# One modulation segment of a two-layer mixer and MoE kernel, made in the routing of layer 0 instead of between its gates

## The chip, the cores and the metric

The kernel runs on one core of one Trainium2 chip. The metric is the device time of one execution in microseconds; three executions of the kernel before are given, and one profiled execution, from which all rows are read. The engines are PE (TensorE; PEld is its weight load), DVE (VectorE), ACT (ScalarE), POOL (GpSimd) and SP (SyncE, whose queue issues most of the loads).

## The reference, cut to what matters

Two layers work on 512 latent tokens and 256 context tokens of width 1024. In each, adaptive modulation rows (six segments of 1024, one row for the latent tokens and one for the context) shift, scale and gate what the layer does.

```python
for l in range(2):
    with_ctx = l < 1
    mod   = silu(c)     @ w_mod[l] + b_mod[l]      # w_mod[l] is 1024 x 6144
    mod_c = silu(c_ctx) @ w_mod[l] + b_mod[l]
    sh1, sc1, gt1, sh2, sc2, gt2 = split(mod, 6)   # csh1 ... cgt2 likewise
    h, hc = modulate(x, sh1, sc1), modulate(ctx, csh1, csc1)
    y = sum(sigmoid(h @ w_gate[n] + b_gate[n]) * (branch_n(h @ w_in) @ w_branch[n])
            for n in A, B, C, D) @ w_out           # four kinds of attention
    x = x + gt1 * y                                # with_ctx: the same for ctx
    h2 = modulate(x, sh2, sc2)
    x = x + gt2 * hier_moe(h2)                     # 32 experts, 2 for each token
return rmsnorm(x)
```

Segment (1, 5) of the kernel is `gt2` of layer 1, the gate on its mixture of experts. It is read only when layer 1 combines its experts. The context row of layer 1 is needed for the segments 0 and 1 alone.

## The kernel before

Both layers are one program, run stage by stage: the norm and the first two modulation segments (to about 45 us), the attention branches and gates of layer 0 (to 820 us), its merge, output projection and routing (to 945), its experts (to 1260), and the same for layer 1.

In the attention stage two streams of work go into one instruction order. The main items are the branches, in the order B, A, C, D: loads of `w_in`, splits of each weight tile into a high part `wH` on ACT and a low part `wL` on DVE (lines 278 and 279), projections, scores, softmax, transposes (line 259). The other stream, `gates()`, fills in: 32 columns of gates, each with a 512 KB load of `w_gate` (line 288), a split, 24 matmuls for each token group, a tanh, and a store of `th` (line 1252). A planner, `Flow`, models the engines and chooses at each step between a main item and the next piece of fill; of the fill it takes so much that its modelled work stays under `FILL` times that of the main items (0.8 in layer 0, 0.4 in layer 1). Its choices are fixed before the kernel runs: each engine executes its list in order.

At every odd column `gates()` first makes a modulation segment with `mod_seg(l, q, new)`: a load of the bias row into a tile `mrow` (line 400), eight loads of `w_mod` of 512 KB each into tiles `wmod` (line 405), for each of them four matmuls of 256 columns, with the two silu columns as weights, replicated to 32 (line 254: `mat`; the four run in separate column groups of the array), a DVE addition of the bias (line 413), and writes of the row to a DRAM tile `modd` by POOL's queue (line 418). Between two of the eight groups the planner may put main work. The tiles come from the pool `gslot`, six buffers that the gates share.

The output projection has its own `Flow`, with ratio 0.0. For each tile of 128 tokens it makes four quarters of the projection, transposes, router logits (`post`), and after every three tiles `route`, which picks experts and counts them. Its weights and the merged rows are in the pool `slot`, 30 buffers. The last of `route` writes indices (`at`, L1909, then the owners' weights, L1921), and `overflow_list` counts the experts whose tokens exceed 64 (`nbb`, `ovJ`, `ovv`, `ovvb`; L1727 to L1753) into `LE`, `LR` and `nover`. A hardware loop then runs from `nover`, and its entry waits for all engines and queues. 26 expert tiles `e` are loaded ahead of it (L1699, also from `slot`). After it the experts run in pairs (L1782).

Of the kernel before, what the change touches and what calls it, by code (L numbers as in the profile page):

```python
# [19 lines left out]
D = 1024  # L20
# [125 lines left out]
class Flow:  # L146
# [13 lines left out]
    def use(self, cls, after):  # L160
        self.used.append((cls, after))
# [74 lines left out]
class Build:  # L236
# [157 lines left out]
    def mod_seg(self, l, q, new, use=None):  # L394

        nc = self.nc
        sl = self.gslot(name="mrow")
        bias, row = sl[:, :256], sl[:, 256:512]
        b = self.a["b_mod"][l, q * D:(q + 1) * D]
        nc.sync.dma_start(bias, bass.AP(tensor=b.tensor, offset=b.offset, ap=[[256, 4], [0, 32], [1, 256]]))  # L400
        yield 0.0, ("bk",)
        ps = self.bank()
        for k in range(8):
            w = new(name="wmod")
            nc.sync.dma_start(w, self.a["w_mod"][l, q, k])
            for g in range(4):
                self.mat(ps[32 * g:32 * g + 32, :256], self.sc[:, k, :], w[:, g * 256:(g + 1) * 256],
                         start=k == 0, stop=k == 7, tile_position=(0, 32 * g))
            if k < 7:
                yield self.LT["mod"], ()  # L410
        if self.fl:
            self.fl.use("bk", self.LT["gacc"])
        nc.vector.tensor_tensor(row, ps[:, :256], bias, op=ALU.add)
        if use:
            use(row)
        else:
            for g in range(4):
                nc.gpsimd.dma_start(self.modd[l][:, q * D + g * 256:q * D + (g + 1) * 256],
                                    row[32 * g:32 * g + 2, :])

    def mix_rows(self, l):

# [109 lines left out]
    def dense(self, x, sh, A):  # L532

        f = self.fl = Flow(NSLOT - 14 if self.l else NSLOT - 10, FILL[self.l])
        if self.l == 0:
# [689 lines left out]
    def gates(self):  # L1225
        nc, l, f = self.nc, self.l, self.fl
        bg = self.tiny.tile([128, 4, 8], F32, name="bg", tag="bg")
        nc.gpsimd.dma_start(bg, self.a["b_gate"][l])
        hb = self.tiny.tile([128, 4, 8], F32, name="hb", tag="hb")
        nc.vector.tensor_scalar(hb, bg, 0.5, None, op0=ALU.mult)  # L1230
        segs = [(0, q) for q in range(2, 6)] + [(1, q) for q in range(6)] if l == 0 else []
        for i in range(32):
            n, m = ORDER[i // 8], i % 8
            if segs and i % 2 == 1:
                yield from self.mod_seg(*segs.pop(0), self.gslot)
            H, L = self.load_split(self.a["w_gate"][l, n, m].rearrange("p k n -> p (k n)"), self.gslot, eng=GE and nc.gpsimd)
            v = lambda s: s.rearrange("p (k n) -> p k n", k=8)
            H, L = v(H), v(L)
            for t0, tn in [(0, 512), (512, 256)][:1 + self.wc]:
                yield 0.0, ("bk", "norms") if t0 else ("bk",)  # L1240
                G = self.bank()
                for k in range(8):
                    a, b = (self.hsl(z, k, t0, tn) for z in range(2))
                    for x, y in ((H, a), (H, b), (L, a)):
                        self.mat(G[:, :tn], x[:, k], y, start=k == 0 and y is a and x is H,
                                 stop=k == 7 and x is L)
                    if k < 7:
                        yield 0.0, ()
                f.use("bk", self.LT["gacc"])
                th = self.sm.tile([128, 512], F32, name="th", tag="th", bufs=2)  # L1250
                nc.scalar.activation(th[:, :tn], G[:, :tn], AF.Tanh, scale=0.5, bias=hb[:, n, m:m + 1])  # L1251
                nc.sync.dma_start(self.thd[n][m, :, t0:t0 + tn], th[:, :tn])
            self.gate[8 * n + m].done, self.gate[8 * n + m].t = True, f.clk
        self.give(12)
# [87 lines left out]
    def out_proj(self):  # L1342
        nc, l = self.nc, self.l
        f = self.fl = Flow(NSLOT, 0.0)
# [31 lines left out]
        def quarter(i, t):  # L1376
            W, x, cs = self.wo[i], self.x1[t], slice(i * 256, (i + 1) * 256)
            ps = self.bank()
            terms = [(ysl(0, k, t), ysl(1, k, t), W(0, k), W(1, k)) for k in range(8)]
            early = i == 0 and t in order[:4]  # L1380
            if early:
                self.mm3(ps[:, :256], terms[:4], True, False)
                f.use("bk", 9000.0)
                yield 3600.0, ()
                b = f.busy["bk"]
                b[b.index(max(b))] = f.clk
            else:
                self.mm3(ps[:, :256], terms[:4], True, False)
            f.use("bk", self.LT["x"])
            self.mm3(ps[:, :256], terms[4:], False, True)  # L1390
            tmp = self.t1("xtmp")
            nc.vector.tensor_tensor(tmp, ps[:, :256], gt1[t // 4][:, cs], op=ALU.mult)
            nc.vector.tensor_tensor(x[:, cs], x[:, cs], tmp, op=ALU.add)

        def turn(t):
            hT[t] = self.gslot(name="xT").rearrange("p (k n) -> p k n", k=8)
            h2, ss = part[t] = self.gslot(name="h2"), self.tiny.tile([128, 2], F32, name="ss2", tag="ss2", bufs=2)
            tp = self.sps()
            f.use("S", self.LT["h2T"])
            for k in range(6):  # L1400
                self.tr(tp[:, k * 128:(k + 1) * 128], self.x1[t][:, k * 128:(k + 1) * 128])
            nc.scalar.activation(hT[t][:, 0:6], tp[:, :768].rearrange("p (k n) -> p k n", k=6), AF.Copy)
            nc.scalar.activation(h2[:, :768], self.x1[t][:, :768], AF.Square, scale=1.0 / 32.0, accum_out=ss[:, 0:1])
            return
            yield
# [11 lines left out]
        def post(t, lt):  # L1417
            x, r = self.x1[t], t // 4
            h2, ss = part[t]
            nc.scalar.activation(h2[:, 768:], x[:, 768:], AF.Square, scale=1.0 / 32.0, accum_out=ss[:, 1:2])  # L1420
            rs = self.rstd(ss[:, 0:1], 1, add=ss[:, 1:2])
            if not H2L:
                norm2(t, h2, rs)
            yield self.LT["x2"], ("bk",)
            tp = self.transposed([x[:, k * 128:(k + 1) * 128] for k in (6, 7)])
            f.use("bk", self.LT["tps"])
            nc.scalar.activation(hT[t][:, 6:8], tp, AF.Copy)
            yield self.LT["h2"], ("bk",)
            lg = self.bank()
            f.use("bk", self.LT["tps"])  # L1430
            for k in range(8):
                self.mat(lg[:, :36], hT[t][:, k], wA[r][:, k], start=k == 0, stop=k == 7)
            nc.vector.scalar_tensor_tensor(lt, lg[:, :36], rs[:, 0:1], cst[r], op0=ALU.mult, op1=ALU.add)
            if H2L:
                norm2(t, h2, rs)
# [12 lines left out]
        for n in RB[l]:  # L1448
            lt = self.sm.tile([128, n, 36], F32, name="lt", tag="lt")
            posts = []  # L1450
            for i in range(n):
                u = order[t + i]
                q3 = f.item(quarter(3, u), deps=[load], need=("bk",))
                tr = f.item(turn(u), deps=[q2[u]], lat=self.LT["x1"], need=("S",))
                posts.append(f.item(post(u, lt[:, i]), deps=[tr, q3, con]))
                f.items += ([] if QM else [q2[u]]) + [tr, q3, posts[-1]]
            t += n
            f.items.append(f.item(self.route(t - n, n, lt, t == self.nt), deps=posts))
        f.run()
        self.fl = None  # L1460

# [513 lines left out]
class Half:  # L1975
# [43 lines left out]
    def v(self, j, t):  # L2019
        return self.V[:, t, 0:64] if self.kind == "g" else self.V[:, t, 64 * j:64 * j + 64]  # L2020
# [15 lines left out]
NT2 = 3  # L2036
GE = False
UPOOL = (3,)
FILL = (0.8, 0.4)
WINDOW = 80  # L2040
ORDER = (1, 0, 2, 3)
PEX = 2
# [27 lines left out]
```

## Time and profile before

| | us |
|---|---|
| three runs | 2195.0, 2189.59, 2190.14 (median 2190.14) |
| the profiled execution | 2185.97 |
| its span, from the first to the last record | 2184.2 |
| granted TensorE clock over the span | 0.97 of 2.4 GHz |
| PE busy | 2020.9 (93%) |

The profiled execution is 4.17 us under the median, and its span leaves out 1.8 us of it. A granted clock of 1.0 in a window is the level of 2.4 GHz, 0.5 that of 1.2 GHz; a value between tells how much of the window had which.

### The profile page before, as it was taken

How to read it: one execution, taken by the hardware profiler on the slowest of the kernel's cores; microseconds unless marked ns; L12 is line 12 of the kernel's file. 1: busy time of each engine (PE TensorE's matmuls, PEld its weight loads, DVE VectorE, ACT ScalarE, POOL GpSimd, SP SyncE). 2: the span in 40 equal slices, each digit the busy share in tenths (PEclk: the TensorE clock that was granted, in tenths of full speed). 3: DMA queues.
4: the chain of work that ended last, by engine and by line, in shares of the span. 5: the costliest groups of instructions: out<-in, count | busy, mean ns of one | idle time of the engine just before them, and what ended most of it. 6: DMA issues, size and time to landing. Idle time of an engine off the chain costs nothing. (4 is left out here: it accounts for less than half of the span.)

```text
span 2184.2 us, 33259 instructions
## 1 busy us (share of the span) xinstructions
PE 2020.9 (93%) x12573; PEld 1483.2 (68%) x12573; DVE 1255.9 (58%) x2695; ACT 799.1 (37%) x1825; POOL 249.8 (11%) x291
## 2 busy tenths in 40 slices
PE   5999999998999998879999979999999999699997
PEld 3878778777788888834444468877877779644443
DVE  3465444245553564677777766565465476656555
ACT  4454554344453221212222235565455432211122
POOL 1101000011100132330000031000020001200000
PEclk8999999999999999889999989999999999799999
DMA  7453542543334656679999423212222478799991
GB/s 285 148 180 102 169 163 81 172 130 100 126 92 134 204 191 212 242 257 393 369 366 365 174 78 100 63 57 88 63 66 77 135 250 288 243 392 409 410 405 68
DMA packets 152931, 428.48 MB, mean 196 GB/s; under 512 B 31488, under 2 KB 43152, under 8 KB 152768
## 3 DMA queue, kind: packets, MB, share of 16 engines
q1 hardware_dynamic: 139744, 392.79, 50.7%
q0 software_dynamic: 11584, 28.29, 4.0%
q10 hardware_dynamic: 1440, 5.24, 0.6%
q8 instruction: 101, 1.65, 0.3%
q14 instruction: 62, 0.51, 0.1%
HBM read 396.28 MB, written 36.78 MB: 198 GB/s over the span
## 5 line engine op out<-in xcount | busy, mean ns | idle before, releaser
L254 PE MATMUL bk<-hT,wH 128*128 128x512 f32 (+1 forms) x1824 | 501.2, 362 | 3.5 <-ACT wH L278 3.1
L254 PEld LDWEIGHTS bk<-hT,wH 128*128 128x128 f32 x1824 | 314.0, 190 | 54.6 <-issue 9.7
L254 PE MATMUL bk<-hT,wL 128*128 128x512 f32 (+1 forms) x912 | 325.6, 357 | 6.9 <-DVE wL L279 6.9
L1841 DVE TENSOR_TENSOR x<-x,sps 128x1024 f32<-128x1024 f32 x166 | 195.4, 1217 | 100.4 <-PE sps L1840 99.8
L1782 PE MATMUL bk<-e,xT 128*64 128x512 f32 x1056 | 245.0, 602 | 0.0
L279 DVE TENSOR_TENSOR wL<-wraw,wH 128x1024 fp32r<-128x1024 f32 (+1 forms) x128 | 157.4, 1234 | 93.6 <-ACT wH L278 59.0
L254 PE MATMUL bk<-wH,hT 128*128 128x256 f32 (+1 forms) x960 | 203.2, 301 | 5.6 <-ACT wH L278 3.6
L254 PEld LDWEIGHTS bk<-hT,wL 128*128 128x128 f32 x912 | 172.9, 190 | 35.2 <-DVE wL L279 10.3
L278 ACT ACTIVATE wH<-wraw 128x1024 fp32r<-128x1024 f32 (+1 forms) x132 | 137.8, 1048 | 136.2 <-DMA wraw<-in_w_gate_dram 45.1
L1782 PEld LDWEIGHTS bk<-e,xT 128*64 128x64 f32 x1056 | 71.9, 138 | 142.3 <-issue 124.0
L254 PEld LDWEIGHTS bk<-wH,hT 128*128 128x128 f32 x960 | 160.7, 194 | 8.5 <-ACT wH L278 3.8
L1840 PE MATMUL sps<-yeH,to 128*128 128x512 f32 x332 | 142.1, 428 | 2.8 <-ACT yeH L278 1.4
L254 PE MATMUL bk<-wL,hT 128*128 128x256 f32 (+1 forms) x480 | 143.0, 298 | 0.8 <-DVE wL L279 0.7
L1203 ACT ACTIVATE P<-sps,m 128x768 f32<-128x768 f32 (+3 forms) x160 | 117.7, 737 | 58.2 <-DVE m L1184 43.5
L1221 ACT ACTIVATE pt<-bk 128x384 f32<-128x384 f32 (+1 forms) x288 | 112.5, 436 | 67.7 <-PE bk L259 66.3
L1840 PE MATMUL sps<-yeL,to 128*128 128x512 f32 x332 | 131.2, 395 | 1.7 <-DVE yeL L279 1.7
L259 PE MATMUL bk<-ident,P 128*128 128x128 f32 x720 | 111.4, 279 | 21.7 <-ACT pt L1221 13.7
L1805 PE MATMUL bk<-e,gT 128*64 128x512 f32 x528 | 122.2, 605 | 1.5 <-ACT gT L1798 1.5
L1788 ACT ACTIVATE eth<-bk 128x256 f32<-128x256 f32 x33 | 12.7, 385 | 284.8 <-PE bk L1782 284.8
L1251 ACT ACTIVATE th<-bk,hb 128x512 f32<-128x512 f32 x96 | 59.1, 616 | 155.9 <-PE bk L254 149.6
L259 PEld LDWEIGHTS bk<-ident,P 128*128 128x128 f32 x720 | 81.9, 140 | 50.5 <-ACT pt L1221 22.8
L325 POOL TENSOR_TENSOR rr<-rs,mhalf 128x1 f32<-128x1 f32 (+1 forms) x72 | 52.0, 723 | 547.1 <-DVE rs L321 476.8
(358 smaller groups left out, 3572.8 us busy)
## 6 DMA issues: line engine op xcount, KB each, us to landing
e<-in_w_dram SPq DMA_DIRECT2D x384, 512.0 KB
wmod<-in_w_mod_dram SPq DMA_DIRECT2D x96, 512.0 KB
wraw<-in_w_gate_dram SPq DMA_DIRECT2D x64, 512.0 KB
thd<-th SPq DMA_DIRECT2D x64, 256.0 KB
wraw<-in_w_in_dram SPq DMA_DIRECT2D x28, 512.0 KB
thm<-thd SPq DMA_DIRECT2D x32, 384.0 KB
wraw<-in_w_br_dram SPq DMA_DIRECT2D x16, 512.0 KB
wraw<-in_w_out_dram SPq DMA_DIRECT2D x16, 512.0 KB
```

The source lines that it names most:

```text
L254: return self.nc.tensor.matmul(out, lhsT, rhs, **kw)
L259: return self.nc.tensor.transpose(out, src, self.ident if ident is None else ident)
L278: nc.scalar.activation(H, src, AF.Copy)
L279: (eng or nc.vector).tensor_tensor(L, src, H.bitcast(F32), op=ALU.subtract)
L325: self.nc.gpsimd.tensor_tensor(r[:, :n], o[:, :n], self.mhalf.to_broadcast([128, n]), op=ALU.pow)
L1203: nc.scalar.activation(Pt[:, :n], S[:, lo:768], AF.Exp, scale=-1.0, bias=m, accum_out=sm)
L1221: nc.scalar.activation(PT[gi][:, i0:i0 + w, qi * 128:(qi + 1) * 128], v, AF.Copy)
L1251: nc.scalar.activation(th[:, :tn], G[:, :tn], AF.Tanh, scale=0.5, bias=hb[:, n, m:m + 1])
L1782: nc.tensor.matmul(box["h"][64 * z:64 * z + 64, :], xT(k, z), W(z, k // 2)[:, (k % 2) * 512:(k % 2 + 1) * 512], start=k == 0, stop=k == 7, ...
L1805: nc.tensor.matmul(Y[n][64 * z:64 * z + 64, :], gT[:, k, 64 * z:64 * z + 64], W(z, 4 + k)[:, n * 512:(n + 1) * 512], start=k == 0, stop=k ...
L1840: nc.tensor.matmul(ps[:, c], to[s, t * 128:(t + 1) * 128], w[s, c], start=i == 0, stop=i == 1)
L1841: nc.vector.tensor_tensor(self.x1[t] if out is None else out, self.x1[t], ps, op=ALU.add)
```

## The change

Segment (1, 5) leaves the list of `gates()`, which now makes nine segments in layer 0, not ten. The output projection of layer 0 gets one item more: the same segment, after the last `route`, with its tiles from `slot`. The writes of a row to `modd` are issued as one DMA with four pieces of 1 KB for each row in place of four DMAs with two rows each, and for layer 1 only the rows that are read later: 16 issues in the program (eight for layer 0, four for the segments 0 and 1 of layer 1 and four for its segments 2 to 5) where 40 stood. `FILL` of layer 0 goes from 0.8 to 0.787.

```diff
@@ mod_seg
         if use:
             use(row)
         else:
-            for g in range(4):
-                nc.gpsimd.dma_start(self.modd[l][:, q * D + g * 256:q * D + (g + 1) * 256],
-                                    row[32 * g:32 * g + 2, :])
+            dst = self.modd[l][:, q * D:(q + 1) * D].rearrange("r (g n) -> r g n", g=4)
+            for r in range(2 if l == 0 or q < 2 else 1):
+                nc.gpsimd.dma_start(dst[r], row[r:128:32, :])
@@ gates
-        segs = [(0, q) for q in range(2, 6)] + [(1, q) for q in range(6)] if l == 0 else []
+        segs = [(0, q) for q in range(2, 6)] + [(1, q) for q in range(5)] if l == 0 else []
@@ out_proj
             f.items.append(f.item(self.route(t - n, n, lt, t == self.nt), deps=posts))
+        if l == 0:
+            f.items.append(f.item(self.mod_seg(1, 5, self.slot), deps=posts))
         f.run()
@@ constants
-FILL = (0.8, 0.4)
+FILL = (0.787, 0.4)
```

Lines behind the second edit carry numbers two higher in the changed kernel. In the rows below a name's number tells one buffer from the next, and `x` with a number counts equal instructions in a row.

The first place is SP's queue among the gates of layer 0, where the last segment's tiles are loaded: `wmod` are its weights, `wraw<-in_w_in` a tile for the branches, `wraw<-in_w_gate` one for a gate column, `o` the store of an attention output. Before:

```order
L405 DMA wmod<-in_w_mod_dram 128x1024 x2
L288 DMA wraw<-in_w_in_dram 128x1024
L1147 DMA o_451<-oT 128x256
L405 DMA wmod<-in_w_mod_dram 128x1024 x2
L288 DMA wraw<-in_w_in_dram 128x1024
L288 DMA wraw<-in_w_gate_dram 128x1024 x3
```

and the same store with its neighbours after the change:

```order
L288 DMA wraw<-in_w_gate_dram 128x1024
L1252 DMA thd_464<-th 128x256
L288 DMA wraw<-in_w_in_dram 128x1024
L1147 DMA o_451<-oT 128x256
L288 DMA wraw<-in_w_in_dram 128x1024
L1252 DMA thd_464<-th 128x512
```

The two `wmod` loads that stood between the store of `o` and the next `w_in` tile are gone; the `w_in` tile follows the store at once.

The second place is PE's list at the end of the routing, from the last indices to the loop (`at` is the assignment matrix, `pt2` and `wp` what it is multiplied with, `nover` the loop's bound in a register). Before:

```order
L1909 MATMUL bk_9816<-pt2_8740,at_9575 128x2
...
L1921 MATMUL bk_9914<-wp_8743,at_9575 128x6
L1733 LDWEIGHTS trib_369
L1733 MATMUL bk_9943<-nbb_9941,trib_369 32x64
L1748 LDWEIGHTS oneb_75
L1748 MATMUL bk_9957<-ovvb_9955,oneb_75 128x72
L1608 TENSOR_LOAD nover_9813
```

and after:

```order
L1911 MATMUL bk_9766<-pt2_8663,at_9498 128x2
L254 MATMUL bk_9689<-wmod_9793,silu_81 32x256 x4
...
L254 MATMUL bk_9689<-wmod_9811,silu_81 32x256 x4
L1923 LDWEIGHTS at_9498
L1923 MATMUL bk_9890<-wp_8666,at_9498 128x6
...
L1735 MATMUL bk_9919<-nbb_9917,trib_369 32x64
L1750 LDWEIGHTS oneb_75
L1750 MATMUL bk_9933<-ovvb_9931,oneb_75 128x72
L1610 TENSOR_LOAD nover_9763
```

The last four of the segment's eight groups, 16 matmuls, have come between the last indices and the chain over `nbb` and `ovvb` that ends in the loop's bound; the first four stand further up, three behind the last router logits and one ahead of the last indices.

The third place is DVE's list at the same point (`nb` and `nbb` count the overflow, `ovJ` is made from PE's product with `nbb`, `w` are the owners' weights). Before:

```order
L1729 TENSOR_REDUCE nb_9939<-ovF_9937 32x1
L1731 CAST nbb_9941<-nb_9939 32x64
L1735 TENSOR_SCALAR ovJ_9945<-iota_367,bk_9943 32x11
L1736 TENSOR_TENSOR ovJ_9945<-ovJ_9945,ovF_9937 32x11
```

and after:

```order
L1731 TENSOR_REDUCE nb_9915<-ovF_9913 32x1
L1733 CAST nbb_9917<-nb_9915 32x64
L413 TENSOR_TENSOR mrow_9687<-bk_9689,mrow_9687 128x256
L1928 TENSOR_REDUCE w_9897<-bk_9890 64x1 x2
L1737 TENSOR_SCALAR ovJ_9921<-iota_367,bk_9919 32x11
L1738 TENSOR_TENSOR ovJ_9921<-ovJ_9921,ovF_9913 32x11
```

The bias addition of the segment, and two reductions that stood further up, have come between `nbb` and `ovJ`.

## Rows read from the trace of the kernel before

**Rows 1.** The page's span line and PE's, DVE's, ACT's, POOL's busy time.
```profile
span 2184.2 us, 33259 instructions
...
PE 2020.9 (93%) x12573; PEld 1483.2 (68%) x12573; DVE 1255.9 (58%) x2695; ACT 799.1 (37%) x1825; POOL 249.8 (11%) x291
```

**Rows 2.** Windows: PE, PEld, DVE, ACT, POOL busy; granted clock; DMA share; GB/s.
```profile
45.00:820.00 775.00, 740.26 (x5065) 611.25 (x5064) 390.71 (x931) 341.37 (x825) 83.84 (x114) 0.98 0.43 142
820.00:945.00 125.00, 95.07 (x780) 92.33 (x781) 74.10 (x196) 23.09 (x55) 36.58 (x37) 0.84 0.60 209
```

**Rows 3.** Timeline of PE, 318 to 322 us: start, duration, line, out<-in, count.
```profile
318.86 0.38 PE L259 MATMUL bk<-ident,dup 128*128 128x128 f32 x2
319.08 0.38 PE L259 MATMUL bk<-ident,qr 128*128 128x128 f32 x2
319.39 0.64 PE L254 MATMUL bk<-wmod,silu 128*32 128x256 f32 x8
319.96 0.44 PE L259 MATMUL bk<-ident,dup 128*128 128x128 f32 x2
```

**Rows 4.** Timeline of PE, modulation matmuls back to back, before 46 us.
```profile
26.48 2.92 PE L254 MATMUL bk<-wmod,silu 128*32 128x256 f32 x48
...
34.45 4.75 PE L254 MATMUL bk<-wmod,silu 128*32 128x256 f32 x32 [1.11 <-DMA wmod<-in_w_mod_dram]
```

**Rows 5.** Tile wmod, 545 to 576 us: min/median/max ns, first and last start.
```profile
L254 PE MATMUL bk<-wmod,silu x64: 379/403/636, 547.8 to 573.0; 128*32 128x256 f32 x64
```

**Rows 6.** Around 561 us: SP's issues, ACT's split, PE's wait (sum, times, longest).
```profile
555.93 0.89 SPq L405 DMA_DIRECT2D wmod<-in_w_mod_dram  x2
556.87 0.42 SPq L288 DMA_DIRECT2D wraw<-in_w_in_dram  x1
...
564.02 1.06 ACT L278 ACTIVATE wH<-wraw 128x1024 fp32r<-128x1024 f32 x1 [2.06 <-DMA wraw<-in_w_in_dram]
...
PE bk L254 <- ACT wH L278: 3.6, 1, 3.6
```

**Rows 7.** Waits of PE, 480 to 505 us: sum, times, longest.
```profile
PE bk L254 <- DMA wmod<-in_w_mod_dram: 3.1, 3, 1.5
PE bk L254 <- ACT wH L278: 1.6, 1, 1.6
```

**Rows 8.** Windows, with the columns of rows 2.
```profile
502.00:506.00 4.00, 3.89 (x20) 3.71 (x21) 1.80 (x5) 2.00 (x4) 0.00 (x0) 0.60 0.10 33
562.00:571.00 9.00, 5.12 (x26) 3.55 (x26) 3.76 (x6) 2.81 (x4) 0.80 (x1) 0.62 0.32 107
...
904.00:913.00 9.00, 8.12 (x49) 8.12 (x49) 4.11 (x14) 2.59 (x8) 0.72 (x1) 0.62 0.17 61
921.00:946.00 25.00, 8.04 (x76) 5.64 (x77) 19.98 (x86) 2.84 (x10) 8.20 (x8) 0.52 0.50 183
```

**Rows 9.** Timeline of PE, end of the routing to the first experts.
```profile
936.46 0.23 PE L1733 MATMUL bk<-nbb,trib 32*32 32x64 bf16 x1 [1.66 <-DVE nbb L1731]
939.26 0.24 PE L1748 MATMUL bk<-ovvb,oneb 32*128 32x72 bf16 x1 [2.57 <-DVE ovvb L1746]
...
942.21 1.97 PE L1690 MATMUL bk<-ident,xg 128*128 128x128 f32 x8 [2.71 <-issue]
944.11 7.78 PE L1782 MATMUL bk<-e,xT 128*64 128x512 f32 x32
```

**Rows 10.** Tiles mrow and modd by line; timeline of POOL.
```profile
L413 DVE TENSOR_TENSOR mrow<-bk,mrow x12: 415/421/426, 32.4 to 573.7; 128x256 f32<-128x256 f32 x12
...
L418 POOL DMA_DIRECT2D modd<-mrow x40: 499/503/824, 93.7 to 576.1; - x40
...
188.78 2.02 POOL L418 DMA_DIRECT2D modd<-mrow  x4
```

**Rows 11.** Timeline of SP's queue, the expert loads ahead of the loop.
```profile
851.95 10.90 SPq L1699 DMA_DIRECT2D e<-in_w_dram  x6
...
875.80 44.11 SPq L1699 DMA_DIRECT2D e<-in_w_dram  x20
```

## The prediction, made before the changed kernel ran

> **What bounds the kernel now.** The page first [rows 1]: PE is busy for 2020.9 of 2184.2 us, and no other engine comes near that. So the next view is the time in which PE is not busy, by stage [rows 2]. In the attention and gates of layer 0 (45 to 820 us) PE is busy for 740.26 of 775.00 us at a granted clock of 0.98: it is the bound there, what is taken from its list shortens the stage, and only 34.7 us of idle time lie in it. In the merge's end, the output projection and the routing (820 to 945) it is busy for 95.07 of 125.00 at 0.84: 29.9 us idle, most of it behind the router's chain on DVE. The change carries work from the first of these stages into the second. Whether that pays is a question about two places: what a group of modulation matmuls costs between other work at 550 us, and whether it fits into idle time of PE at 922 to 942.
>
> **a) Eight groups leave the gates.** The timeline of PE at 319 us gives the price of one group that stands alone [rows 3]. Two transposes start at 318.86, two more at 319.08, so two take 0.22. After the pair at 319.08 the next transposes would start at 319.30; with a group of modulation matmuls between, they start at 319.96, 0.66 later. (The group's eight records are two for each of its four matmuls.) The eight groups of segment (1, 5) lie between 547.8 and 573.0, 64 records [rows 5], with other work between them, so 8 x 0.66 = 5.3 us. Back to back they would be cheaper: 48 records, six groups, take 2.92 us [rows 4], and less the 0.64 of one group [rows 3] that is 2.28 for five, 0.456 each, 3.6 for eight. The groups here are apart, so I take **-5.3**; bounds -3.6 and -5.3.
>
> **b) The stall that the segment's loads make.** Around 561 us PE waits 3.6 us for a split `wH`, ACT itself waited 2.06 us for the load of that `w_in` tile, and SP issued this load at 556.87, right behind two `wmod` loads of 0.89 us [rows 6]. They belong to segment (1, 5), and in the new order of SP's queue (the first place above) none stands there. The load took 564.02 - 556.87 = 7.15 us; with 1 MB less ahead of it, it should be in time or nearly so. ACT's 2.06 us is what a load can be blamed for; the rest of PE's wait is ACT and the score chain. After the wait PE ran at a granted clock of 0.62 from 562 to 571, 5.12 us busy [rows 8]: at most half of it, 2.6 us, was lost to the low level. I take **-2.0**; bounds 0 (something else holds PE there) and -4.7 (2.06 + 2.6).
>
> **c) The segment in the routing.** PE's new list (the second place) puts three groups behind the last router logits and one ahead of the last indices, where PE waits for DVE: 17 of the 25 us from 921 to 946 are idle [rows 8]. These four cost nothing while their loads are there. They are eight loads of 512 KB issued right behind the four of `w_out`, far ahead of 922. The other four groups stand between the last indices and `nbb`'s matmul, on the chain to the loop. The timeline [rows 9]: PE took `nbb` at 936.46 after 1.66 us idle, so it was free at 934.80. Four groups at the low clock take 4.75 us [rows 4], and low it is: 0.52 from 921 to 946 [rows 8]. They end at 939.55, 3.1 behind 936.46. DVE then adds the bias, 0.42 us [rows 10], ahead of `ovJ` (the third place): 3.5. Everything behind moves with it: `ovvb` (2.57 us of waiting), `nover`, the loop's entry, the first experts' transposes at 942.21. So **+3.5**. Bounds: at full clock four groups take 4 x 0.456 = 1.8, of which 1.66 are idle anyway, +0.2 and the 0.42 of the addition, **+0.6**; or the 1.66 are not there, because the matmuls wait for a tile, +4.75 without an overlap, **+4.8**. A tile is the less likely trouble: its buffers come free when the output projection has read `w_out`.
>
> The bias load waits in SP's queue for a tile of `gslot`, and behind it stand the last ten expert loads. Before, 26 were issued from 851.95 to 919.9 [rows 11]. Those ten now go out only near 922 and later, and some wait for the tiles of `wmod` themselves. What covers this: layer 0 starts with the pair at 944.11 [rows 9], which needs the first tiles, not the last; and the loop's entry holds everything until 942. I take **0**. If the cover went, the price would be one tile's issue and landing late, under 7.15 us by the load of [rows 6].
>
> **d) Fewer writes.** The 40 issues cost POOL 0.503 us each [rows 10]; 24 fewer are 12 us of POOL, which is busy for 11% of the span [rows 1]. It is hidden, but for work of POOL that queues behind four in a row (2.02 us at 188.78 [rows 10]); PE there has other work. **0**, at best -1. The write's new shape is not in the trace; its result is read much later, except for segments 0 and 1 of layer 0, which don't go this way.
>
> **e) The new order of the stage.** With `FILL` at 0.787 and a segment less, the planner's list for the whole stage is another one. Nothing in it is more or less work; what can differ is the number of places where a load or a split is late. The trace shows one such cluster, at segment (1, 4): from 480 to 505 us PE waits 3.1 us for `wmod` and 1.6 for a split [rows 7], and then runs at 0.60 for 3.89 busy us [rows 8], of which 40% or 1.6 us is lost: 6.3 us in all. I take **0**, with ends of -6.3 and +6.3 for one cluster less or more. This term is the widest, and I have no row that would decide its sign.
>
> **The sum**: -5.3 - 2.0 + 3.5 + 0 + 0 + 0 = -3.8. Against the profiled execution (2185.97, a span of 2184.2 and 1.8 around it) that is 2182.2. The median of the runs shown is 4.2 above that execution, so for a median I forecast 2190.1 - 3.8 = **2186.3**. About 0.3%, 6.6 us, is what a measurement of this kernel can tell from no change; the forecast lies within it.
>
> **The rivals.**
> *One starved cluster less* (chance 0.30). The places at 485 and 561 us both have `wmod` loads ahead of something urgent [rows 6, 7]; a list with a segment less and a lower ratio may let the first of them vanish too. Then -3.8 - 6.3 = -10.1: 2180.0. Against it: the ratio falls by under 2%, and segment (1, 4) is still there.
> *The routing takes it all back* (0.17). The stall at 561 stays in another form (0 for b), and the four groups cost their full 4.75: -5.3 + 4.75 = -0.6, 2189.6. For it speaks that the chain from `nbb` to the loop has no slack at all [rows 9].
> *Two new starved clusters* (0.11), the one on the other side. Two columns of gates whose split comes late, as at 561 [rows 6], with b) gained nowhere: -5.3 + 3.5 + 2 x 6.3 = +10.8, 2200.9. It decides from 6.6 + 1.8 = 8.4 us of new stall on; one cluster alone gives +4.5. Against it: in 775 us PE now idles only 34.7 [rows 2].
> *The clock wakes in the routing* (0.08). From 921 to 946 PE is granted 0.52, and a window from 904 on shows 0.62 though PE is busy for 8.12 of 9.00 us in it [rows 8]. Were the 16 matmuls enough to bring back 2.4 GHz, the transposes and the first expert matmuls from 942.21 to 946 would run at the high level: at most half of 3.8, 1.9 us. The sum would be -5.7, 2184.4. Beside this: the Trainium skill ("TensorE: Matmul & The Clock Gate", its part on the HAM clock gate) says that sustained work of PE brings the full clock and idling takes it away. The trace agrees that it falls with idling; that it would rise for so short a piece, the rows of 904 to 913 speak against.
>
> The forecast itself, within 3 us or so of 2186.3, has 0.34.
>
> **How the numbers follow.** Faster by over 0.3%: the cluster less, 0.30, and some of the forecast where b) and c) fall to their good ends (-5.3 - 4.7 + 0.6 = -9.4), 0.04: 0.34. Slower by over 0.3%: 0.11. The rest, 0.55, is no change that can be told. The range has to leave out no more than 0.2: below it goes past the cluster less (2180.0) by the difference of b)'s bounds, some 4, to 2176; above past the lost gain (2189.6) by one cluster of 6.3 and a little, to 2197, which leaves out the slower rival. The forecast's own range is 2181 to 2190: the sum with the bounds of b) and c) in it, -9.4 to -0.5.
>
> **What the changed kernel's profile would show.** For a): the columns around 550 to 570 us without modulation matmuls, and the stage shorter by about 5. For b): no wait of 3.6 for `wH` there, idle time of PE from 45 to 820 near 31 and not 35. For c): 16 modulation matmuls (32 records) that start when the last indices have been taken, at a granted clock near 0.5, 4.7 us long; `nbb`'s matmul no longer idle before it, and 4.7 to 5.2 us from the last indices to it, not 1.7; the first expert 3.5 us later after the last indices than before. For the expert loads: no wait of PE for `e`. For e): the sum of PE's waits in the stage; new ones over 1 us for `wH`, `wmod` or `P` say that the list moved the starved places. The prediction is wrong if that sum differs by more than 6 us, if the four groups are not in the way of `nbb`, or if the last expert loads hold up the first pairs.

## The result

| | us | ratio to before, 95% interval |
|---|---|---|
| before, four runs | 2190.28 (2189.59 to 2195.0) | |
| the changed kernel, four runs | 2203.72 (2200.63 to 2209.81) | 1.0066 (1.0049 to 1.0083) |
| its profiled execution | 2200.63, span 2198.8 | |

The change made the kernel 13.4 us slower; 2186.3 was forecast, with a range to 2197. Over all its runs beside the experiments the kernel before took between 2180.2 and 2196.9 us, so a few microseconds of any single profile are chance. Where the time went is therefore read by stages, over all kernels of the study.

The page of the changed kernel answers to [rows 1]: the span and the busy time of each engine.

```profile
span 2198.8 us, 33194 instructions
...
PE 2031.7 (92%) x12573; PEld 1491.6 (68%) x12573; DVE 1255.4 (57%) x2695; ACT 796.4 (36%) x1825; POOL 237.3 (11%) x267
```

PE has the same 12573 matmuls, the span 14.6 us more. Only 3.8 of these are idle time of PE (163.3 us became 167.1); for the same matmuls PE is busy 10.8 us longer. That is the clock for the most part: half of PE's busy time at the lower level, which is the cost if the same work takes half the time at the upper one, adds up to 33.7 us before and 44.9 after. POOL has the 24 instructions and 12 us less that d) gave it. The two windows of [rows 2], of the changed kernel:

```profile
45.00:820.00 775.00, 736.57 (x4990) 611.70 (x4991) 388.55 (x925) 337.91 (x824) 71.05 (x89) 0.98 0.42 136
820.00:945.00 125.00, 103.24 (x842) 96.73 (x840) 70.60 (x178) 22.84 (x53) 36.14 (x38) 0.85 0.67 231
```

Up to 820 us PE got through 75 matmul records fewer (4990, before 5065), and 64 of these are the segment's: it stands about where it stood before, though it has less to do. The table has the stages of all kernels, from the start of one matmul to the start of another in the timelines of their profiles, in us, as differences of rounded times (the first column is a time). "Logits" is the last router-logit matmul; "first expert" and the end of "experts" are the first and the last matmul of the experts' first product, `bk<-e,xT`, so that the last pair's second product lies in the column behind:

| kernel | first output projection | to last logits | to first expert | experts of layer 0 | to layer 1's first projection | rest |
|---|---|---|---|---|---|---|
| before | 811.8 | 110.2 | 22.2 | 302.0 | 28.8 | 909.2 |
| changed | 812.7 | 113.5 | 28.1 | 302.3 | 33.1 | 909.0 |
| e1 writes merged alone | 810.7 | 112.2 | 22.3 | 300.6 | 28.9 | 911.1 |
| e2 FILL 0.787 alone | 829.7 | 113.5 | 22.3 | 302.4 | 31.3 | 910.7 |
| e3 segment moved alone | 810.0 | 110.8 | 29.0 | 304.9 | 32.3 | 910.3 |
| e4 moved, writes | 807.8 | 110.3 | 28.3 | 303.5 | 31.0 | 910.4 |
| e5 changed, 18 tiles ahead | 814.7 | 113.7 | 25.0 | 307.3 | 31.0 | 909.8 |
| e6 changed, after first route | 813.2 | 109.9 | 23.5 | 301.2 | 28.9 | 909.4 |
| e7 e8 with 18 tiles | 806.9 | 108.1 | 22.3 | 306.7 | 31.2 | 911.2 |
| e8 after first route, FILL 0.8 | 810.6 | 111.5 | 24.6 | 299.8 | 29.7 | 913.1 |
| e9 the same, 0.794 | 797.5 | 109.9 | 24.6 | 300.9 | 28.9 | 909.3 |
| e10 the same, 0.806 | 801.6 | 110.1 | 23.0 | 302.0 | 28.8 | 909.1 |
| e11 the same, 0.812 | 802.0 | 107.6 | 24.1 | 300.0 | 28.9 | 908.6 |
| e12 no segment, 0.8 | 811.3 | 113.7 | 22.1 | 302.4 | 28.9 | 905.9 |

In the changed kernel's profile: +1.0 up to the output projection, where a) and b) promised -7.3; +3.3 in the output projection; +5.9 at the routing's end; +0.3 in the experts; +4.3 behind them; -0.2 in the rest. The +3.3 in the output projection are the clock: PE is busy at the lower level for 9.7 us there before and for 15.9 after, and half of the difference is 3.1. It is not the segment's doing: e2 and e12, which have no segment there, have 17.5 and 16.2.

**The routing's end.** The timeline of PE in the changed kernel answers to [rows 9]:

```profile
924.32 2.34 PE L254 MATMUL bk<-wr,xT 128*128 128x36 f32 x16 [0.49 <-ACT xT L1402]
926.59 2.79 PE L254 MATMUL bk<-wmod,silu 128*32 128x256 f32 x24
...
935.34 1.08 PE L254 MATMUL bk<-wmod,silu 128*32 128x256 f32 x8
...
939.42 3.64 PE L254 MATMUL bk<-wmod,silu 128*32 128x256 f32 x32
...
943.17 0.20 PE L1735 MATMUL bk<-nbb,trib 32*32 32x64 bf16 x1
946.35 0.20 PE L1750 MATMUL bk<-ovvb,oneb 32*128 32x72 bf16 x1 [2.98 <-DVE ovvb L1748]
952.44 1.97 PE L1692 MATMUL bk<-ident,xg 128*128 128x128 f32 x8 [5.88 <-DMA e<-in_w_dram]
954.33 1.98 PE L1784 MATMUL bk<-e,xT 128*64 128x512 f32 x4
```

The groups lie as the order said: 24 records in idle time, 8 ahead of the last indices, 32 between them and `nbb`, 3.64 us long. From the last router logits to `ovvb` it takes 946.35 - 924.32 = 22.03. In the kernel before the logits' row reads:

```profile
919.94 2.39 PE L254 MATMUL bk<-wr,xT 128*128 128x36 f32 x16 [0.49 <-ACT xT L1402]
```

939.26 [rows 9] - 919.94 = 19.32, so the matmuls and the addition cost +2.7, where c) said +3.5. But then PE waits for 5.88 us, where it waited for 2.71 [rows 9], and the row names the load of an expert tile. SP's queue there:

```profile
923.96 12.69 SPq L1701 DMA_DIRECT2D e<-in_w_dram  x7
935.90 5.00 SPq L1701 DMA_DIRECT2D e<-in_w_dram  x4
```

DVE's first instruction behind the entry:

```profile
952.34 0.17 DVE L1884 COPY er<-LE 128x2 f32<-128x2 f32 x1 [5.27 <-DMA e<-in_w_dram]
```

and three windows, with DMA share and GB/s at the end:

```profile
948.00:950.00 2.00, 0.00 (x0) 0.00 (x0) 0.00 (x0) 0.00 (x0) 0.00 (x0) 0.50 0.86 349
950.00:951.00 1.00, 0.00 (x0) 0.00 (x0) 0.00 (x0) 0.00 (x0) 0.00 (x0) 0.50 0.32 131
951.00:952.00 1.00, 0.00 (x0) 0.00 (x0) 0.00 (x0) 0.00 (x0) 0.00 (x0) 0.50 0.03 12
```

Every engine stands still from 948 on while data come in at 349 GB/s, until the transfers end at about 951; the first instruction behind the loop's entry runs at 952.34. Before, the last expert load was issued by 920 [rows 11], and the loads were long done when the entry was reached. The eight `wmod` tiles stand in front of the expert tiles, in SP's queue and in the ring of 30 buffers, so the last loads went out at 935.9 to 940.9.

**Behind the experts of layer 0.** A place the prediction did not look at. DVE's rows of the last pair, before:

```profile
1249.04 0.41 DVE L1791 TENSOR_TENSOR gg<-eth,bk 128x256 f32<-128x256 f32 x1
1249.37 1.22 DVE L431 SCALAR_TENSOR_TENSOR mixrow<-mixrow,gmix 128x1024 f32<-128x1024 f32 x1
```

and of the changed kernel:

```profile
1259.54 1.22 DVE L431 SCALAR_TENSOR_TENSOR mixrow<-mixrow,gmix 128x1024 f32<-128x1024 f32 x1
1260.68 0.41 DVE L1793 TENSOR_TENSOR gg<-eth,bk 128x256 f32<-128x256 f32 x1
```

PE's wait there (sum, times, longest):

```profile
PE bk L1799 <- DVE gg L1793: 2.8, 1, 2.8
```

and the window behind it, with its granted clock ahead of the last two columns:

```profile
1261.00:1267.00 6.00, 5.85 (x16) 2.54 (x18) 3.58 (x4) 2.27 (x3) 0.00 (x0) 0.50 0.30 87
```

A product for layer 1's rows, 1.22 us, has moved ahead of `gg`, for which PE waits: 2.8 us, and 1.6 before. After it the clock is at its lower level, and 5.85 busy us run at half speed. The segment moved out of one ring of buffers into another (nine tiles fewer from `gslot` among the gates, eight more from `slot`), and DVE's order 300 us later is another one. What in the move changes it, no run shows: e6 below takes the same tiles from the same rings and has the old order.

**The attention stage.** PE's longest waits from 45 to 812 us, before and then changed:

```profile
PE bk L254 <- DVE wL L279: 5.7, 5, 2.6
PE bk L254 <- ACT wH L278: 5.1, 2, 3.6
...
PE bk L259 <- DVE xnh L988: 1.2, 1, 1.2
```

```profile
PE bk L254 <- DVE wL L279: 6.8, 4, 3.5
PE bk L254 <- ACT wH L278: 5.1, 2, 3.2
...
PE bk L259 <- DVE xnh L988: 4.6, 3, 2.4
```

The 3.6 us of [rows 6] are gone, and a wait of 3.2 for another `wH` (at 401 us) and one of 2.4 for `xnh` (at 190 us) have come; the longest for `wL` (at 721 us) has grown from 2.6 to 3.5. In sum: from 45 us to the output projection PE idled 34.0 us before and 37.6 after, and lost half of its busy time at the lower level, 9.1 and 11.2. Without both, 723.7 us of work have become 718.9: the segment's 4.8 us did leave.

### The profile page after: what moved, and what is told of

The parts are those of the page before. It is cut to its first block, busy times and chain, and to the rows that moved or that the text cites. A ratio compares the mean times of both kernels' runs of the same rounds, so it can differ in the third digit from the quotient of the medians.

```text
span 2198.8 us, 33194 instructions
## 1 busy us (share of the span) xinstructions
PE 2031.7 (92%) x12573; PEld 1491.6 (68%) x12573; DVE 1255.4 (57%) x2695; ACT 796.4 (36%) x1825; POOL 237.3 (11%) x267
## 5 line engine op out<-in xcount | busy, mean ns | idle before, releaser
L254 PEld LDWEIGHTS bk<-hT,wL 128*128 128x128 f32 x912 | 173.6, 190 | 36.6 <-DVE wL L279 11.3
L259 PE MATMUL bk<-ident,P 128*128 128x128 f32 x720 | 110.4, 279 | 22.1 <-ACT pt L1221 14.4
```

The costliest lines, as they stand in the source:

```text
L254: return self.nc.tensor.matmul(out, lhsT, rhs, **kw)
L259: return self.nc.tensor.transpose(out, src, self.ident if ident is None else ident)
```

## The experiments

Three edits in one change: first each alone. Each ratio is to the kernel before as it ran beside the experiment (medians 2189.37 for e1 to e4, 2189.66 for e5 to e8, 2188.64 for e9 to e12). **e1**, the writes:

```diff
-            for g in range(4):
-                nc.gpsimd.dma_start(self.modd[l][...], row[32 * g:32 * g + 2, :])
+            for r in range(2 if l == 0 or q < 2 else 1):
+                nc.gpsimd.dma_start(dst[r], row[r:128:32, :])
```

> Only the writes to modd are merged (16 issues for 40); the order of every other instruction is that of before. Theory A (the loss has two parts: at the routing's end the loop entry waits for expert loads that eight modulation tiles ahead of them have pushed back, with four groups of matmuls on the chain, 5.8 us together; and the planner's new list for the attention stage, which took back the 7.3 us that were to be gained there): no change, within 1 us of before. Rival B (the merged, strided write lands later, 4.9 us after its issue for 1.6, and holds up who reads modd or POOL's queue): slower by 3 us or more.

Measured 2186.83, ratio 0.9988 (0.9977 to 0.9998). Rival B is out, and its premise does not hold in general: the 4.9 us were one write of the changed kernel among the expert loads; the 16 writes of e1 land 1.7 us after their issue in the median, the 40 of before 1.6. It is a little faster, 2.5 us; that is more than the 1 us at best of d), but the interval (0.4 to 5.0 us) reaches down to it. Which wait became shorter the single profiles don't show.

**e2**, the planner's ratio:

```diff
-FILL = (0.8, 0.4)
+FILL = (0.787, 0.4)
```

> Only FILL goes to 0.787; all ten segments stay between the gates, the writes stay as before. Theory A: the new list costs what the changed kernel lost in the attention stage: slower by 3 to 8 us, all of it before 830 us, the routing's end as before (last router logits to first expert 24 us). Rival C (the list is neutral, and the loss is the move's alone): within 2 us of before.

2204.09, ratio 1.0070 (1.0056 to 1.0084): +14.7. In its profile, the slowest of its six runs (2211.68), the output projection begins 17.9 later (829.7 for 811.8), and the routing's end is untouched (22.3). Rival C is out, and theory A named too small a price. The longest waits in its attention stage:

```profile
PE bk L254 <- ACT wH L278: 6.6, 3, 2.7
PE bk L259 <- DVE P L1208: 5.2, 3, 4.0
PE bk L259 <- DVE xnh L988: 4.6, 3, 2.4
```

40.6 us idle and 15.7 lost to the clock, against 34.0 and 9.1; another 4.7 are in the work itself, 728.4 against 723.7. Most of that lies in the 416 products with `V` (`bk<-pt,V`), in which PE is busy for 51.98 us, before 48.44; why they take longer in this list, no run shows.

**e3** and **e4**, the segment alone, and with the writes:

```diff
-... [(1, q) for q in range(6)] if l == 0 else []
+... [(1, q) for q in range(5)] if l == 0 else []
@@ out_proj
+        if l == 0:
+            f.items.append(f.item(self.mod_seg(1, 5, self.slot), deps=posts))
```

> Only the segment is moved (FILL 0.8, writes as before). Theory A: the routing's end as in the changed kernel, 30 us from the last router logits to the first expert where before has 24.2, so +5.8; the attention stage shorter by 5 to 7 if its list has no new stalls; in sum -2 to +1 on before, 11 to 15 below the changed kernel. Rival C: the whole loss is here, +10 or more.

> The changed kernel with FILL 0.8: segment moved and writes merged. The order of PE is that of the kernel with the move alone. Theory A: within 1 us of the move alone. Rival B: slower than it by 3 us or more.

e3: 2199.13, ratio 1.0053 (1.0038 to 1.0068), +9.8; e4: 2195.34, 1.0029 (1.0016 to 1.0041). The routing's end is that of the changed kernel in both (29.0 and 28.3, before 22.2), and so is the place of `gg`. The move is a loss by itself, nearly the +10 of rival C and not the -2 to +1 of theory A: the attention stage gave back 2 to 4 us of the 7, the routing's end took 6 to 7 and the stretch behind the experts 2 to 3.5. The writes gain again, 3.8, with intervals that just touch. With FILL 0.787 on top it is the changed kernel: 8.4 more.

**e5** tests the loop's entry: fewer tiles ahead of it.

```diff
-PRE = (26, 26)
+PRE = (18, 26)
```

> The changed kernel with 18 expert tiles loaded ahead of the loop in layer 0 in place of 26. Theory A (the loop's entry waits until the last of the expert loads, issued at 940.6 us, has landed at about 951): PE's idle time ahead of the first experts' transposes falls from 5.88 us to about 3, as before's 2.71, and from the last router logits to the first expert it takes 25 us, not 28.1; the whole is 3 us faster, if the pairs then don't wait for their tiles. Rival D (the entry waits for the segment's own write to modd, issued at 943.85 with 4.9 us to landing): the idle time stays at 4.5 us or more.

2198.51, ratio 1.0043 (1.0029 to 1.0058), 5.2 less than the changed kernel, where 3 were expected. The timeline of PE at the entry:

```profile
948.52 0.20 PE L1750 MATMUL bk<-ovvb,oneb 32*128 32x72 bf16 x1 [2.99 <-DVE ovvb L1748]
951.47 1.97 PE L1692 MATMUL bk<-ident,xg 128*128 128x128 f32 x8 [2.75 <-issue]
```

The wait is 2.75 us again: the entry waits for the expert loads. D is out by the changed kernel's own trace: its write, issued at 943.85, landed 4.9 us later, at 948.8, and the entry came at 952.34. That the pairs wouldn't suffer was wrong: the experts take 307.3 for 302.3, and DVE's order among them has changed too.

**e6** has the segment at another place in the output projection, after the first of the two routes:

```diff
             f.items.append(f.item(self.route(t - n, n, lt, t == self.nt), deps=posts))
-        if l == 0:
-            f.items.append(f.item(self.mod_seg(1, 5, self.slot), deps=posts))
+            if l == 0 and t < self.nt:
+                f.items.append(f.item(self.mod_seg(1, 5, self.slot), deps=posts))
```

> The changed kernel with the segment's item after the first of the two routes in place of the last; all eight groups then stand ahead of the last router logits, where PE has work. Theory A: 3.6 to 5.3 us more up to the last router logits, and from there to the first expert 22 to 25 us, not 28.1. DVE's order at the end of the experts is that of before again (gg ahead of the first product for the next layer's rows), so PE's wait for gg is 1.6 us, not 2.8, and the clock does not fall there: 29 us from the last expert matmul of layer 0 to layer 1's first projection, not 33.1. In sum 3 to 7 us faster than the changed kernel. Rival E (those 4 us at the end of the experts are a matter of when the clock happens to fall, not of gg's place): 31 to 33 us there again.

2187.67, ratio 0.9994 (0.9978 to 1.0011): 16 us under the changed kernel by one line. PE at the routing's end:

```profile
923.35 1.07 PE L254 MATMUL bk<-wmod,silu 128*32 128x256 f32 x16
...
938.08 0.23 PE L1735 MATMUL bk<-nbb,trib 32*32 32x64 bf16 x1 [1.93 <-DVE nbb L1733]
940.88 0.24 PE L1750 MATMUL bk<-ovvb,oneb 32*128 32x72 bf16 x1 [2.57 <-DVE ovvb L1748]
944.73 1.97 PE L1692 MATMUL bk<-ident,xg 128*128 128x128 f32 x8 [3.62 <-DVE er L1884]
```

DVE at the end of the experts:

```profile
1250.68 0.41 DVE L1793 TENSOR_TENSOR gg<-eth,bk 128x256 f32<-128x256 f32 x1
1251.01 1.22 DVE L431 SCALAR_TENSOR_TENSOR mixrow<-mixrow,gmix 128x1024 f32<-128x1024 f32 x1
```

and PE's wait for it:

```profile
PE bk L1799 <- DVE gg L1793: 1.6, 1, 1.6
```

The chain to the loop is bare, its entry costs 0.9 more than before, `gg` is first again, and the stretch behind the experts takes 28.9, not 33.1.

The 0.9 at the entry show that it waits for any queue. The last transfers ahead of it are no expert loads here, but POOL's gather of `xg`, the routed tokens' rows, issued at 938.35. In the changed kernel SP's queue (q1) alone moves more than two packets from 948.5 to 952 us, in e6 POOL's (q0) from 940 to 944.4 (packets, MB, share):

```profile
q1 hardware_dynamic: 178, 0.61, 42.8%
```

```profile
q0 software_dynamic: 186, 0.48, 36.2%
```

In e8 to e11 POOL's queue is the last one too, and PE's wait at the entry is 3.3 to 5.1 us.

In the nine profiles with a wait of 1.6 for `gg` the stretch behind the experts takes 28.8 to 29.7, but for e2 (31.3); with 2.8, 31.0 to 33.1 (changed, e3, e4). (With 18 tiles ahead, e5 and e7, the order there is a third one, and it takes 31.0 and 31.2.) The clock does not follow the order. These are the windows right behind the wait, of e2 with its 1.6 and of e4 with its 2.8:

```profile
1271.50:1275.00 3.50, 3.50 (x10) 1.64 (x10) 2.84 (x4) 1.33 (x2) 0.00 (x0) 0.51 0.09 23
```

```profile
1254.40:1260.40 6.00, 5.32 (x23) 2.09 (x23) 5.27 (x6) 2.90 (x4) 0.00 (x0) 1.00 0.26 87
```

The clock is low behind the short wait and high behind the long one. So of the 4.3 us the order accounts for the 1.2 of the longer wait; for the rest rival E holds, and what sets the clock there is open.

The dearer half is a surprise: up to the last logits e6 takes 109.9, less than the changed kernel's 113.5 without the segment in it. There PE idled for 11.3 us against 14.4 and was busy at the lower level for 6.2 against 15.9. It is the same in all six kernels with the segment after the first route: 10.3 to 11.5 us idle and 3.3 to 9.4 at the lower level, where the eight others have 13.3 to 15.1 and 9.7 to 17.5. The segment fills idle time there; that the fewer pauses keep the clock up is likely, but was not tested by itself.

**e7** and **e8** are these edits with FILL 0.8, with 18 and with 26 tiles ahead of the loop.

> The last but one change with FILL 0.8 and 18 tiles ahead of the loop. Theory A: the two gains together, 5 to 8 us below the kernel with segment and writes moved and FILL 0.8 (2195.3), so 2187 to 2190: no better than before with the writes merged alone (2186.8). Rival: the pairs starve for tiles, slower than 2195.

> Segment after the first route, writes merged, FILL 0.8, 26 tiles. Theory A: from 2195.3 (the segment after the last route) down by 3 to 6 us, to 2189 to 2192. Rival F (a segment costs the same wherever it stands in the output projection): 2194 to 2197.

e8: 2183.56, ratio 0.9979 (0.9965 to 0.9994), faster than before and 11.8 under e4, which has the same list in the attention stage: rival F is out, and theory A's gain too small. e7: 2189.80, 1.0004 (0.9992 to 1.0017): the entry is free (22.3), the experts 7 us longer, so 26 tiles are right.

**e9 to e12**: three more ratios on e8, and e8 without the segment.

> Segment after the first route, writes merged, FILL 0.794 (0.8 gave 2183.6, 0.787 gave 2187.7). Theory G (each ratio gives another list, whose stalls lie by chance within some 8 us either way, with no trend): between 2180 and 2196, not necessarily between the two neighbours. Rival M (a lower ratio delays the gates, and the time rises steadily as it falls): 2184.5 to 2187.

> The same with FILL 0.806. Theory G: between 2180 and 2196. Rival M: 2180 to 2182.5, lower than at 0.8.

> The same with FILL 0.812. Theory G: between 2180 and 2196. Rival M: 2176 to 2181, lower again.

> Segment (1, 5) is left out: its row is written from the sums of segment (1, 4), so the last gate of layer 1 has other values. Writes merged, FILL 0.8, the list of the attention stage that of the kernels with the segment moved. It tells what the segment costs in its two places. Theory A (after the first route it takes 3.6 to 5.3 us of PE and pushes the expert loads back; after the last route it costs 6 us behind the last logits and up to 4 at the end of the experts, by gg's place): 2178 to 2181, that is 3 to 6 us under the kernel with the segment after the first route and 14 to 17 under the one with it after the last. Rival F (the segment is nearly free after the first route, hidden in PE's waits): 2182 to 2184.

| FILL, segment after the first route | us | ratio, 95% interval |
|---|---|---|
| 0.787 (e6) | 2187.67 | 0.9994 (0.9978 to 1.0011) |
| 0.794 (e9) | 2173.78 | 0.9926 (0.9900 to 0.9953) |
| 0.8 (e8) | 2183.56 | 0.9979 (0.9965 to 0.9994) |
| 0.806 (e10) | 2173.90 | 0.9928 (0.9903 to 0.9953) |
| 0.812 (e11) | 2177.32 | 0.9951 (0.9936 to 0.9966) |
| 0.8, no segment (e12) | 2182.05 | 0.9966 (0.9953 to 0.9978) |

No steady trend, and 14 us between neighbours. All three new ratios came out under theory G's 2180: of it only the missing order held, not the size. Rival M is right at 0.812 alone; a steady rise is out. Windows up to 600 us, e9 and then e12, with the list of 0.8:

```profile
45.00:600.00 555.00, 537.20 (x3832) 441.87 (x3833) 275.23 (x761) 270.22 (x698) 37.53 (x56) 0.99 0.39 131
```

```profile
45.00:600.00 555.00, 530.85 (x3756) 434.87 (x3755) 269.55 (x743) 266.44 (x684) 37.35 (x56) 0.99 0.39 129
```

e9 has 76 matmul records more behind it at 600 us: 6.4 us less idle, and 27.4 idle in the whole stage for 35.0. The segment itself, against e12, which leaves it out: 1.5 us after the first route (e8), 13.3 after the last (e4). The 1.5 are not clear of noise, the two intervals overlap for the most part; e12 lies 0.05 us inside rival F's range and 1 us above theory A's, which does not decide between them.

## Why the prediction was wrong

- **a)** held: 723.7 us of work became 718.9, -4.8 for -5.3, and 715 to 719 in all kernels with the segment out of the gates.
- **b)** had the place right and the gain wrong. The wait at 561 us went; others came, so that the stage's idle time rose from 34.0 to 37.6. A stall that is taken away in a list that a planner makes anew can't be booked apart from e).
- **c)** held in its mechanism: +2.7 for +3.5. Its four groups took 3.64 us at a granted 0.50, not the 4.75 of [rows 4].
- The step on the later expert loads failed: "What covers this ... the loop's entry holds everything until 942. I take **0**". The entry is no cover, it is who waits: it let nobody through before the last of the loads had landed. That cost 5.88 - 2.71 = 3.2 us, and e5 shows it. That the entry waits for all queues was said of the kernel before; the step did not draw the consequence. The upper end given there (7.15) would have held it, but it was not in the sum or in a rival.
- **d)** was right in sign and probably too small: -2.5 and -3.8 in two comparisons, for 0 to -1, with intervals that reach to about its bound.
- **e)** is the largest miss. I took 0 with ends of 6.3 either way from one cluster of stalls. e2 shows +14.7 for the ratio alone, e4 and the changed kernel +8.4 for it with the segment moved, e9 to e11 gains of 6 to 10 on e8. The three edits don't add up one by one (-2.5, +14.7 and +9.8 for a change of 13.4); each meets another list. The row I had gave the price of one cluster, not how many a new list makes or removes.
- **The clock** is in the sum at one stall only, in b), and e) gives it 1.6 us in a cluster. In the profile it is the larger part of the loss, 11.2 us in all: PE's idle time grew by 3.8. No row of before told how much of it another list would bring.
- **Not seen at all**: `gg` behind a product for the next layer, 1.2 us, and the clock in that stretch, together +4.3 in the profile. The swap stands in DVE's order of the changed kernel, far from the places of the diff, and the prediction priced only those.
- The rivals: the slower one gave 2200.9 by two clusters among the gates, and 2203.7 came, but by other ways, some 6 us at the routing's end, some 4 behind the experts, 3 of clock in the output projection, and an attention stage that gained nothing. The clock's rival was half right, as these windows of the changed kernel show:

```profile
933.00:943.00 10.00, 6.86 (x86) 3.41 (x85) 6.70 (x36) 1.05 (x4) 2.11 (x2) 0.50 0.94 329
943.00:947.00 4.00, 0.57 (x9) 0.33 (x5) 3.32 (x14) 0.00 (x0) 0.65 (x1) 0.93 1.03 417
947.00:954.00 7.00, 1.56 (x8) 1.57 (x8) 1.73 (x14) 0.41 (x1) 0.07 (x1) 0.50 0.45 180
```

The clock did come back to 2.4 GHz, at 943, when the matmuls were over; PE then idled, and the experts began at 1.2 GHz all the same. The Trainium skill ("TensorE: Matmul & The Clock Gate", its part on the HAM clock gate) has sustained work raise the clock and idling lower it; these three rows, 0.50, 0.93 and 0.50, agree.

Open: why the merged writes gain 2.5 to 3.8 us, why the products with `V` take longer in e2, what puts `gg` second, and what sets the clock behind it and in the output projection.

## What to carry to other kernels

Work put into idle time is only free if nothing behind it waits for everything: at a loop entry that waits for the transfers under way, a load that is pushed back so far that it is still under way there is waited for, whoever needs it. The same segment cost 1.5 us, hardly to be told from nothing, one route earlier and 13.3 us here. And a ratio that feeds a planner is no dial: five values within some 3% gave 2174 to 2188 us without a steady trend, so it must be tried again after each change, and an edit must be judged over several of them; e9, with the segment after the first route and 0.794, is 0.7% under the kernel before (interval 0.5 to 1.0).

## What the runs showed of the hardware

The entry of the loop comes 1 to 1.6 us behind the end of the last transfers, whichever queue they are in: they end at 951.3 and DVE goes on at 952.34 in the changed kernel (SP's queue), at 943.0 and 944.52 in e6 (POOL's). Where none is under way, PE idles for 2.6 to 2.75 us behind `ovvb` (before, e1, e2, e5, e7, e12). A segment put behind the last route changed the order on DVE 300 us later; behind the first route it did not. PE's clock ran at 0.50 for 5.85 busy us behind a wait of 2.8 us in the changed kernel, and at 1.00 behind the same wait in e4; behind one of 1.6 at this place it ran at 0.51 in e2 and at 1.00 before. The length of this one wait does not decide. A write of four pieces of 1 KB lands 1.7 us after its issue in the median (e1), one of 2 KB 1.6 (before).
